# Padding three groups of matmul operand tiles by 32 bytes each, in a two-block transformer kernel

## The chip, the cores and the metric

The kernel runs on one core of a Trainium2 chip. The metric is the device time of one execution in microseconds (us). TensorE (PE) does the matmuls and loads its stationary operands (PEld), VectorE (DVE) and ScalarE (ACT) do the work on elements, SyncE (SP) issues the DMAs.

## The reference, cut to what matters

Two blocks of two layers each over 512 tokens of width 1024, all in float32. The first block's layers have forgetting, dilated and banded attention with gated branches; the second block's have a differential-attention and pooling mixer or a convolution mixer, then cross attention to 256 memory tokens and an MLP of width 4096. Nearly all of the work is matrix products of this form:

```python
u = jnp.einsum('bsd,dc->bsc', h, w_in[layer])          # first block, 6660 columns
x = x + jnp.einsum('bsd,de->bse', merged, w_out[layer])
...
proj = h @ w_in                                         # second block's mixers
q = (h @ wq).reshape(B, S, X_HEADS, X_HEAD_DIM)         # cross attention
a = jax.nn.relu(h @ w1)                                 # MLP
return (a * a) @ w2
```

## The kernel before

Every float32 operand of a product is split into two halves, a rounded high one and the rest as a low one, and a product of 128 rows of the contraction takes three matmuls: high weight by high input (line 310), high weight by low input (line 311), low weight by high input (line 312). In the usual form the weight's halves are the stationary operand (128 by 128) and the activation's halves are the moving one (128 partitions by 512 tokens); one output of 128 columns takes 8 such groups of three, one for each 128 of the 1024 rows, and all 24 matmuls add into one tile `ps_acc`.

```python
308  def mm3(self, ps, lh, ll, rh, rl, start, stop):
310      mm(ps, lh, rh, start=start, stop=False)
311      mm(ps, lh, rl, start=False, stop=False)
312      mm(ps, ll, rh, start=False, stop=stop)
...
330  def fm_into(self, ps, hi, lo, xh, xl, ks, n=S, ...):
331      for i, k in enumerate(ks):
332          c = slice((k - w0) * P, (k - w0 + 1) * P)
333          self.mm3(ps[:, :n], hi[:, c], lo[:, c], xh[k][:, :n], xl[k][:, :n], ...)
```

The weights come by DMA into `raw`, ScalarE rounds them into `whi` (line 304), and VectorE writes the rest into `wlo` (line 305); each of these has two buffers of 128 by 1024. The tiles that hold activations come from pools of their own, by `tl(tag, ...)`:

- `xhi` and `xlo`, 8 tiles each: the halves of the normalised input of a layer (lines 54 to 57). They are the moving operand of 208 weight units, 24 matmuls each: in the first block 22 units a layer for queries, keys and gates of the heads and 24 for the branch gates; in the second 12 for the even mixer, 24 for the odd one, 16 for cross attention, 64 for the MLP's first product. Of them 124 run in plain loops (36 of the branch gates, the odd mixer, the MLP) and 84 are woven between the steps of attention.
- `y`, 16 tiles, and `mg`, 16 tiles: pools that hold what goes into the second product of a layer. Where the halves are `split(..., "y", "y")`, the three matmuls of a group take y, y, y (384 groups: the branches, the two mixers' and cross attention's output products). In the MLP's second product they are `split(r, "y", "mg")` and the matmuls take y, mg, y (496 groups of 512 tokens; the last 16 groups run in halves of 256). In the first block's output product all come from mg (128 groups).
- `mg` also holds keys and values of attention and the halves of the memory, of 256 tokens; the keys are completed by DMAs from one half of the partitions to the other (lines 589 and 590).

In the products by tokens (`tm_task`, line 349) the roles are turned round: the weight's halves move, and 128 columns of an activation tile are the stationary operand, from `xhi` and `xlo` in 168 matmuls of 512 columns and from `mg` in 192.

A tile of 512 float32 takes 2048 bytes in each partition, and one of 1024 takes 4096; both are multiples of 256. So all tiles of one pool begin at the same byte modulo 256. By the order in which the pools lie in the memory, `raw`, `xhi`, `xlo`, `whi`, `wlo`, `nt`, `gt` and `RB` begin at 128, `mg`, `qk` and `cs` at 192, and `y`, `yt`, `pth` and `ptl` at 64. Slices of 128 columns (512 bytes) inside a tile begin at the same byte modulo 256 as the tile.

The order of the matmuls is written out by the program: plain loops for the large products, and in the stretches of attention a weave (lines 217 to 236) that puts the next matmuls of a list of tasks between the steps of the heads.

Of the kernel before, what the change touches and what calls it, by code (L numbers as in the profile page):

```python
# [33 lines left out]
            gt=4, yt=1, cs=2, nt=3, sz=2, RB=2, small=16, wide=5)  # L34


class Norm:
    """Root-mean-square norm whose per-token factor is applied after the product."""

# [31 lines left out]
    def finish(self, row=True, square=False):  # L71
        """The factors come in two steps, each behind the next product that is emitted."""
        self.steps = [self.per_token] + [self.per_row] * (row or square)
        self.square = square
        self.kr.hooks = list(self.steps)
        return self
# [32 lines left out]
class Head:  # L109
    """One head's steps by stage (scores, values, the rest), each at a place in its period of the weave."""  # L110

# [6 lines left out]
class JointNorm(Norm):  # L118
    """Two norms on end: x <- norm(x) gf, then norm(x) g, from sums over x and over x gf."""

# [36 lines left out]
class Kernel:  # L157
# [15 lines left out]

# [1 line left out]
    def task(self, label, cost, gen, *aps):  # L175
        """aps: the weights that the task takes, in their order."""
        self.work.append([label, cost, gen])
        self.plan += aps
        self.prepare_ahead()
# [7 lines left out]
    def step(self):  # L187
        """The next product of the first task; false where its operands are not there yet."""
        w = self.work[0]
        try:  # L190
            c = next(w[2])
        except StopIteration:
            self.work.pop(0)
            return True
        if c is None:
            return False
        w[1] -= c
        self.due -= c
        return True
# [38 lines left out]
    def tl(self, tag, dt=F32, shape=(P, S)):  # L238
        self.n += 1
        return self.pool.tile(list(shape), dt, tag=tag, name=f"{tag}_{self.n}", bufs=BUFS[tag])  # L240

# [41 lines left out]

# [1 line left out]
    def load(self, ap):  # L285
# [28 lines left out]
    def pv(self, ps, v, hi, lo, start, stop):  # L314
        """The values' halves lie side by side in one stationary tile, or in two tiles."""
        if len(v) == 2:
            return self.mm3(ps, v[0], v[1], hi, lo, start, stop)
        mm = self.nc.tensor.matmul
        mm(ps, v[0], hi, start=start, stop=False)
        mm(ps, v[0], lo, start=False, stop=stop)  # L320

    def stack_v(self, vt, acc, rs):
        """Values of four heads of one token tile: the halves of each one side by side."""
        nc = self.nc
        v = vt.rearrange("p (h c) -> p h c", c=P)
        hi, lo, src = v[:, :, :64], v[:, :, 64:], acc.rearrange("p (h c) -> p h c", c=64)
        nc.scalar.activation(hi, src, AF.Identity, scale=rs)
        nc.vector.scalar_tensor_tensor(lo, src, rs, hi.bitcast(F32), op0=ALU.mult, op1=ALU.subtract)
# [56 lines left out]

# [1 line left out]
    def rstd_tm(self, acc, n, scale, times=None, more=None):  # L387
# [17 lines left out]
    def row_form(self, rs, n):  # L405
        """The per-token factors along the free axis, in every partition."""
        nc, nt = self.nc, n // P
        hi, lo = self.sm(nt, F32R), self.sm(nt, F32R)
        nc.vector.tensor_copy(hi, rs)
        nc.vector.tensor_tensor(lo, rs, hi.bitcast(F32), op=ALU.subtract)  # L410
        ps = self.psum("t")
        for i in range(nt):
            for part in (hi, lo):
                nc.tensor.matmul(ps[:, i * P:(i + 1) * P], part[:, i:i + 1].to_broadcast([P, P]), self.identR,
                                 start=part is hi, stop=part is lo)
        return ps
# [5 lines left out]

# [1 line left out]
    def lowest(self, out, ps, bias, nm):  # L424
        """out = -(ps + bias) and the lowest of each row."""
        self.nc.vector.tensor_tensor_reduce(out, ps, bias, -1.0, HUGE, op0=ALU.add, op1=ALU.min, accum_out=nm)  # L426

    def causal_tile(self, i, qt, kt, bias, tag=None):
        """exp(s - max) of query tile i and the reciprocals of its sums."""
        nc, mm = self.nc, self.nc.tensor.matmul  # L430
        n = P * (i + 1)
        q = slice(i * P, (i + 1) * P)
        bias, masked = bias
        ps = self.psum("s")
        mm(ps[:, :n], qt[:, q], kt[0][:, :n], start=True, stop=False)
        mm(ps[:, :n], qt[:, q], kt[1][:, :n], start=False, stop=masked)
        if not masked:
            mm(ps[:, n - P:n], self.identB, self.bandB[:, P:], start=False, stop=True)
        nm, den, r = self.sm(1), self.sm(1), self.sm(1)
        p = self.tl(tag) if tag else self.tl(f"P{i}", F32, (P, n))  # L440
        self.lowest(p[:, :n], ps[:, :n], bias, nm)
        nc.scalar.activation(p[:, :n], p[:, :n], AF.Exp, scale=-1.0, bias=nm, accum_out=den)  # L442
        nc.vector.reciprocal(r, den)
        return p, r

    def causal(self, qt, kt, bias, v, done):
        """The steps of one causal head; qt, kt, bias and v are called when they are needed."""
        pr = []

        def score(i):  # L450
            p, r = self.causal_tile(i, qt(), kt(), bias(i))
            n = P * (i + 1)
            self.nc.scalar.activation(p[:, :n], p[:, :n], AF.Identity, scale=r)
            pr.append(p)

        return self.places(score), self.causal_values(pr, v, done)
# [4 lines left out]
    def causal_values(self, pr, v, done):  # L461
        """out^T[:, q] over all keys; v(j): the stationary values of key tile j."""
        nc = self.nc
# [25 lines left out]
    def band(self, qt, kt, sink, v, done):  # L489
        """The steps of one head of banded attention with a sink."""  # L490
        nc, mm = self.nc, self.nc.tensor.matmul
# [64 lines left out]

# [1 line left out]
    def z_gate(self, ap, nm):  # L558
        """z * (1 + tanh(z / 2)), twice silu(z)."""
        nc = self.nc  # L560
# [9 lines left out]
    def stack_q(self, q):  # L570
        """Queries of two heads: the halves of each one on end, over the whole contraction."""
        nc = self.nc
# [7 lines left out]
    def stack_k(self, k, tag="mg"):  # L580
        """Keys of two heads: each half of each one twice on end."""
        nc = self.nc
# [32 lines left out]
    def join(self, yt, ps, r):  # L615
        """The products of the values' two halves are added up."""
        rows = slice(64 * r, 64 * r + 64)
# [3 lines left out]
    def first_layer(self, l, nm, nxt, values_a):  # L621
# [7 lines left out]

        # forgetting attention  # L630
        acc = self.run(values_a)
# [40 lines left out]

        # forgetting attention: the decays by key, in every partition
        def decays(h):
# [15 lines left out]

        # dilated mixture and banded attention: rope tables with the norm's factor
        cs = []
# [63 lines left out]

        # gates of the branches: 1 + tanh, twice the sigmoid
        ahead = {}
# [26 lines left out]

        # gates and branches
        if l == 1:
# [73 lines left out]

# [1 line left out]
    def second_block(self, nm):  # L863
# [13 lines left out]
    def mem_norm(self):  # L877
        """In steps, each behind a product."""
        nc = self.nc
# [25 lines left out]
    def mem_halves(self, tag):  # L905
        """The normalised memory in halves: a feature chunk behind each of the next products."""
        nc, M = self.nc, 256
# [35 lines left out]
    def even_prep(self):  # L943
# [5 lines left out]

        # relative bias by distance, the longest first  # L950
        rb, oh, never = self.p1.tile([32, 4], F32, name="rb"), self.tl("nt"), self.tl("nt")
# [16 lines left out]
    def even(self, nm, nxt):  # L968
# [49 lines left out]

        # multi-scale pool
        def pool_in(g):  # L1020
# [59 lines left out]
    def begin(self, begun, w, yh, yl, ks, last):  # L1080
        """The first products of a projection, as far as their operands go."""
        for n in range(2):
# [166 lines left out]
    def finale(self, w, ah, al, nm):  # L1249
        """The last product and the last norm go by groups of tokens."""  # L1250
        nc, k = self.nc, KC - 1
# [40 lines left out]

# [1 line left out]
def _fm(w):  # L1294
    """[K, N] -> [N/128, 128, K]: for each 128 columns, the rows by chunk."""
    k, n = w.shape
# [3 lines left out]
def _tm(w):  # L1300
    """[K, n] -> [K/256, 128, 2 n]."""
    k, n = w.shape
# [115 lines left out]
```

## Time and profile before

| | us |
|---|---|
| median of 2 runs | 2299.23 (2298.43 to 2300.03) |
| span of the profiled execution | 2296.1 |
| PE busy | 2271.1 (99%) |
| PEld busy | 1870.6 (81%) |
| DVE busy | 1283.1 (56%) |
| ACT busy | 990.1 (43%) |

The span goes from the first to the last instruction of the program in the profiled execution; 3.1 us lie between it and the median of the runs. A matmul's own duration in the profile includes the time in which its result drains, while the next one already runs, so the pace of the matmuls is read from start to start.

### The profile page before, as it was taken

What the parts mean: (1) busy time and instruction counts of PE and PEld (TensorE: products, weight loads), DVE (VectorE), ACT (ScalarE), POOL (GpSimd) and SP (SyncE); (2) the same over time, 40 slices, a digit from 0 to 9 for tenths busy, and PEclk for the clock granted to TensorE, in tenths of its full rate; (3) what the DMA queues carried; (4) which work ended last, traced back from release to release, by engine and by line L of the source; (5) the groups of instructions that cost most, each with busy time, mean ns of one, the idle gap of its engine ahead of it and who ended that gap; (6) DMA issues with size and microseconds to landing.
All of it is one profiled execution on the core that took longest, in us unless ns stands there. A gap on an engine that the chain in (4) does not pass through costs nothing.

```text
span 2296.1 us, 27721 instructions
## 1 busy us (share of the span) xinstructions
PE 2271.1 (99%) x10770; PEld 1870.6 (81%) x10770; DVE 1283.1 (56%) x2212; ACT 990.1 (43%) x1672; POOL 19.6 (1%) x21
## 2 busy tenths in 40 slices
PE   8999999999999999999999999999999999999998
PEld 7888888878788888777888888888888887888887
DVE  6688654567885556885455423435455455433433
ACT  6686432366863234654443422333233443422421
POOL 0000000000000000000000000000000000000000
PEclk9999999999999999999999999999999999999999
DMA  5333233243333333323323333333333323333232
GB/s 172 92 106 94 83 95 96 93 119 98 98 104 93 92 106 106 92 83 119 102 92 92 92 101 92 100 93 106 100 93 110 111 83 94 100 93 100 92 101 83
DMA packets 74738, 227.82 MB, mean 99 GB/s; under 512 B 9928, under 2 KB 15692, under 8 KB 74608
## 3 DMA queue, kind: packets, MB, share of 16 engines
q1 hardware_dynamic: 74608, 226.06, 33.2%
q8 instruction: 84, 1.38, 0.2%
q14 instruction: 46, 0.38, 0.1%
HBM read 210.29 MB, written 2.11 MB: 93 GB/s over the span
## 4 chain that ended last, share of the span: by engine, by line
PE 86%; DVE 7%; ACT 4%; issue 1%; DMA 1%; SPq 0%; POOL 0%; DVEq 0%; POOLq 0%; ACTq 0%
PE ps_acc L310 26%; PE ps_acc L312 26%; PE ps_acc L311 26%; DVE wlo L305 2%; ACT whi L304 1%; PE ps_s L310 1%; DVE ptl L381 1%; PE ps_s L311 1%; PE ps_s L312 1%; ACT P L442 1%; PE ps_o L311 1%; PE ps_t L393 1%; PE ps_o L310 1%; PE ps_o L312 1%; DVE P L426 0%
## 5 line engine op out<-in xcount | busy, mean ns | idle before, releaser
L304 ACT CAST whi<-raw 128x1024 fp32r<-128x1024 f32 (+1 forms) x388 | 404.2, 1042 | 1009.7 <-PE ps_acc L311 671.5
L310 PE MATMUL ps_acc<-xhi,whi 128*128 128x512 f32 x1664 | 661.2, 397 | 0.0
L312 PE MATMUL ps_acc<-xhi,wlo 128*128 128x512 f32 x1664 | 650.4, 391 | 0.0
L311 PE MATMUL ps_acc<-xlo,whi 128*128 128x512 f32 x1664 | 649.2, 390 | 0.0
L305 DVE TENSOR_TENSOR wlo<-raw,whi 128x1024 fp32r<-128x1024 f32 (+1 forms) x388 | 470.8, 1213 | 281.4 <-ACT whi L304 280.3
L312 PEld LDWEIGHTS ps_acc<-xhi,wlo 128*128 128x128 f32 x1664 | 312.6, 188 | 66.4
L310 PEld LDWEIGHTS ps_acc<-xhi,whi 128*128 128x128 f32 x1664 | 313.3, 188 | 59.8 <-issue 1.3
L311 PEld LDWEIGHTS ps_acc<-xlo,whi 128*128 128x128 f32 x1664 | 313.2, 188 | 58.7 <-issue 0.5
L312 PE MATMUL ps_acc<-y,wlo 128*128 128x512 f32 (+1 forms) x912 | 356.7, 391 | 1.1 <-DVE wlo L305 1.1
L310 PE MATMUL ps_acc<-y,whi 128*128 128x512 f32 (+1 forms) x912 | 356.5, 392 | 1.2 <-ACT y L383 0.8
L311 PE MATMUL ps_acc<-mg,whi 128*128 128x512 f32 (+1 forms) x784 | 288.8, 368 | 0.0
L312 PEld LDWEIGHTS ps_acc<-y,wlo 128*128 128x128 f32 x912 | 171.2, 188 | 41.3 <-DVE wlo L305 2.4
L310 PEld LDWEIGHTS ps_acc<-y,whi 128*128 128x128 f32 x912 | 171.4, 188 | 40.9 <-ACT whi L304 1.6
L311 PEld LDWEIGHTS ps_acc<-mg,whi 128*128 128x128 f32 x784 | 147.3, 188 | 27.2
L419 DVE TENSOR_TENSOR x<-x,ps_acc 128x512 f32<-128x512 f32 x79 | 54.3, 687 | 192.4 <-PE ps_acc L312 192.4
L311 PE MATMUL ps_acc<-y,whi 128*128 128x512 f32 x384 | 152.0, 396 | 0.0
L1234 DVE SCALAR_TENSOR_TENSOR gt<-ps_acc,RB 128x512 f32<-128x512 f32 x64 | 44.3, 692 | 169.3 <-PE ps_acc L312 167.7
L380 ACT CAST pth<-ps_t 128x512 fp32r<-128x512 f32 (+1 forms) x112 | 58.5, 527 | 72.0 <-PE ps_t L540 22.6
L311 PEld LDWEIGHTS ps_acc<-y,whi 128*128 128x128 f32 x384 | 72.2, 188 | 17.3 <-DVE y L381 0.4
L310 PE MATMUL ps_acc<-mg,whi 128*128 128x512 f32 (+1 forms) x256 | 86.2, 337 | 0.0
L312 PE MATMUL ps_acc<-mg,wlo 128*128 128x512 f32 (+1 forms) x256 | 85.7, 335 | 0.0
L765 DVE TENSOR_TENSOR gt<-ps_acc,RB 128x512 f32<-128x512 f32 x36 | 24.9, 692 | 106.4 <-PE ps_acc L312 106.4
(265 smaller groups left out, 2530.7 us busy)
## 6 DMA issues: line engine op xcount, KB each, us to landing
raw<-in_w_dram SPq DMA_DIRECT2D x128, 512.0 KB, 3.6
raw<-in_w_fm_dram SPq DMA_DIRECT2D x92, 512.0 KB, 3.6
raw<-in_conv_fm_dram SPq DMA_DIRECT2D x24, 512.0 KB, 3.6
raw<-in_w_br_dram SPq DMA_DIRECT2D x16, 512.0 KB, 3.6
raw<-in_w_out_dram SPq DMA_DIRECT2D x16, 512.0 KB, 3.6
raw<-in_xk_dram SPq DMA_DIRECT2D x16, 512.0 KB, 3.6
raw<-in_xv_dram SPq DMA_DIRECT2D x16, 512.0 KB, 3.6
raw<-in_xq_dram SPq DMA_DIRECT2D x16, 512.0 KB, 3.6
```

The lines of the kernel that those rows point to most:

```text
L304: nc.scalar.copy(hi[:, :f], raw[:, :f])
L305: nc.vector.tensor_tensor(lo[:, :f], raw[:, :f], hi[:, :f].bitcast(F32), op=ALU.subtract)
L310: mm(ps, lh, rh, start=start, stop=False)
L311: mm(ps, lh, rl, start=False, stop=False)
L312: mm(ps, ll, rh, start=False, stop=stop)
L380: nc.scalar.copy(hi, src)
L381: nc.vector.tensor_tensor(lo, src, hi.bitcast(F32), op=ALU.subtract)
L393: nc.tensor.matmul(ps[:, i:i + 1], a[:, i * P:(i + 1) * P], self.ones[:, 0:1], start=a is parts[0] and i == 0, stop=a is parts[-1] and i = ...
L419: self.nc.vector.tensor_tensor(self.x[k], self.x[k], ps, op=ALU.add)
L442: nc.scalar.activation(p[:, :n], p[:, :n], AF.Exp, scale=-1.0, bias=nm, accum_out=den)
L765: nc.vector.tensor_tensor(th, ps, nm.RB, op=ALU.mult)
L1234: nc.vector.scalar_tensor_tensor(r, ps, 0.0, nm.RB, op0=ALU.max, op1=ALU.mult)
```

## The change

`tl` allots 520 columns in place of 512 for the tags `xhi`, `y` and `mg`, and gives back the first 512. A tile then takes 2080 bytes, 32 more than a multiple of 256, and the tiles of one pool begin at eight different places modulo 256. The 8 tiles of `xhi` take 256 bytes more in all, those of `y` and `mg` 512 each. These are multiples of 256, so every other tile, and the first tile of each of the three pools, begins at the same byte modulo 256 as before. `xlo`, `whi` and `wlo` stay as they were. Apart from that the change takes out docstrings and comments.

```diff
+STEPPED = ("xhi", "y", "mg")
+
...
     def tl(self, tag, dt=F32, shape=(P, S)):
         self.n += 1
+        if tag in STEPPED:
+            return self.pool.tile([P, S + 8], dt, tag=tag, name=f"{tag}_{self.n}", bufs=BUFS[tag])[:, :S]
         return self.pool.tile(list(shape), dt, tag=tag, name=f"{tag}_{self.n}", bufs=BUFS[tag])
```

## Rows read from the trace of the kernel before

**Rows 1.** The page: busy time by engine, and the span in 40 slices.
```profile
PE 2271.1 (99%) x10770; PEld 1870.6 (81%) x10770; DVE 1283.1 (56%) x2212; ACT 990.1 (43%) x1672; POOL 19.6 (1%) x21
...
PE   8999999999999999999999999999999999999998
...
PEclk9999999999999999999999999999999999999999
```

**Rows 2.** The page: the chain of work that ended last, by engine.
```profile
PE 86%; DVE 7%; ACT 4%; issue 1%; DMA 1%; SPq 0%; POOL 0%; DVEq 0%; POOLq 0%; ACTq 0%
```

**Rows 3.** Groups of matmuls by line and shape: count, busy us, mean ns.
```profile
L310 PE MATMUL ps_acc<-xhi,whi 128*128 128x512 f32 x1664 | 661.2, 397 | 0.0
L312 PE MATMUL ps_acc<-xhi,wlo 128*128 128x512 f32 x1664 | 650.4, 391 | 0.0
L311 PE MATMUL ps_acc<-xlo,whi 128*128 128x512 f32 x1664 | 649.2, 390 | 0.0
...
L310 PE MATMUL ps_acc<-y,whi 128*128 128x512 f32 x880 | 347.4, 395 | 1.2 <-ACT y L383 0.8 <-ACT whi L304 0.4
...
L311 PE MATMUL ps_acc<-mg,whi 128*128 128x512 f32 x624 | 244.2, 391 | 0.0
...
L311 PE MATMUL ps_acc<-y,whi 128*128 128x512 f32 x384 | 152.0, 396 | 0.0
...
L310 PE MATMUL ps_acc<-mg,whi 128*128 128x512 f32 x128 | 50.2, 392 | 0.0
...
L310 PE MATMUL ps_acc<-whi,mg 128*128 128x512 f32 x64 | 25.7, 401 | 0.0
...
L310 PE MATMUL ps_acc<-whi,xhi 128*128 128x512 f32 x56 | 23.0, 411 | 0.0
```

**Rows 4.** Stretches of one kind: length, busy us and count by engine, granted clock, DMA.
```profile
1411.05:1498.10 87.05, 87.05 (x385) 72.07 (x384) 40.44 (x47) 34.15 (x47) 0.00 (x0) 1.00 0.33 97
1600.00:1719.00 119.00, 119.00 (x526) 98.54 (x526) 63.84 (x83) 34.64 (x44) 0.00 (x0) 1.00 0.33 97
1719.28:1764.08 44.80, 44.80 (x193) 35.91 (x192) 24.16 (x30) 16.93 (x23) 0.00 (x0) 1.00 0.33 95
843.64:887.60 43.96, 43.96 (x193) 36.06 (x192) 28.92 (x37) 22.03 (x31) 0.00 (x0) 1.00 0.29 96
1322.30:1410.80 88.50, 88.50 (x384) 71.88 (x383) 25.77 (x25) 17.95 (x18) 0.00 (x0) 1.00 0.32 95
887.60:903.70 16.10, 16.10 (x72) 13.33 (x71) 6.32 (x7) 5.01 (x6) 0.00 (x0) 1.00 0.41 110
```

**Rows 5.** Timeline of PE where one kind of product gives way to another.
```profile
1085.94 0.39 PE L312 MATMUL ps_acc<-whi,mg 128*128 128x512 f32 x1
...
1087.34 0.40 PE L312 MATMUL ps_acc<-whi,mg 128*128 128x512 f32 x1
1087.57 0.40 PE L310 MATMUL ps_acc<-xhi,whi 128*128 128x512 f32 x1
...
1089.19 0.39 PE L311 MATMUL ps_acc<-xlo,whi 128*128 128x512 f32 x1
```

**Rows 6.** Timeline of PE behind a wait, in the first stretch of attention.
```profile
29.79 0.40 PE L311 MATMUL ps_acc<-xlo,whi 128*128 128x512 f32 x1
...
32.10 0.39 PE L312 MATMUL ps_acc<-xhi,wlo 128*128 128x512 f32 x1
```

**Rows 7.** Writers and readers of the padded tiles on other engines and queues.
```profile
L381 DVE TENSOR_TENSOR ptl<-ps_t,pth 128x512 fp32r<-128x512 f32 x76 | 52.2, 687 | 16.1 <-ACT pth L380 15.9
...
L381 DVE TENSOR_TENSOR mg<-gt,y 128x512 fp32r<-128x512 f32 x64 | 44.3, 692 | 2.7 <-ACT y L380 2.7
...
L57 DVE SCALAR_TENSOR_TENSOR xlo<-x,c_vec,xhi 128x512 fp32r<-128x512 f32 x56 | 41.7, 748 | 2.1 <-ACT xhi L56 2.1
...
mg<-mg SPq DMA_DIRECT2D x56, 128.0 KB, 2.7
```

## Prediction

> **What bounds the kernel now.** I read the page's busy times first, then its chain, then the groups of matmuls, and last the pace of the matmuls stretch by stretch. PE is busy for 99% of the span, in every slice but the two ends, at the full granted clock (the 2.4 GHz level) [rows 1], and the chain that ended last is PE for 86% [rows 2]. DVE at 56% and ACT at 43% have slack. So the change can matter only through PE: through the time from one matmul's start to the next.
>
> The groups say how many matmuls of 512 columns there are [rows 3]: 3 x 1664 = 4992 whose moving operands are xhi, xlo, xhi; 384 groups of y, y, y (1152 matmuls); 496 groups of y, mg, y (1488); 128 groups of mg, mg, mg (384). With the weights moving there are 3 x 56 = 168 against xhi and xlo, and 3 x 64 = 192 against mg. Together 8376.
>
> Their durations, 390 to 411 ns, overlap; the pace is in the stretches that hold one kind each [rows 4]. A count there includes one matmul already under way, so the pace is the length over the count less one. At 2.4 GHz 512 columns take 213.3 ns. The x kind runs at 87.05 / 384 = 226.7 ns, and in another layer at 119.00 / 525 = 226.7; y, y, y at 44.80 / 192 = 233.3; mg at 43.96 / 192 = 229.0; y, mg, y at 88.50 / 383 = 231.1; weights against xhi at 16.10 / 71 = 226.8. The weights against mg run at (1087.34 - 1085.94) / 6 = 0.233 us [rows 5]. No idle time stands before these groups [rows 3], and the granted clock is the same in all [rows 4]. What differs is where the tiles begin modulo 256 bytes: weights and x at 128, mg at 192, y at 64. The last two paces are the telling ones: the same moving tiles whi and wlo, 226.8 ns against a stationary tile that begins at the same byte and 233.3 against one that begins 64 bytes further. The pace goes with the place of the moving tile relative to the stationary one: same place 226.7, moving tile 64 bytes further 229.0, 64 bytes less 233.3 (both y against weights and weights against mg).
>
> There is a second effect. After a disturbance the x kind doesn't run at 226.7 at once. From 1087.57 to 1089.19, where x follows another kind, seven spacings take 1.62 us, 231.4 ns each [rows 5]; behind a wait, from 29.79 to 32.10, ten take 2.31 us, 231.0 ns each [rows 6]. So 226.7 is a pace into which a row of like-placed matmuls settles after some ten of them.
>
> **The change part by part.** No instruction, wait or DMA is added or taken away, and no step moves in a queue. Only places change: xhi, y and mg tiles are spread over eight places, whi, wlo and xlo stay at 128. So 24 matmuls of one unit no longer have one relation to their weights: the order goes xhi (one of eight places), xlo (the old place), xhi, and on to the next of eight.
>
> I cost this with the pace of rows in which the relation changes from matmul to matmul. There is one such kind, y, mg, y, at 231.1 ns, and the unsettled stretches of x give 231.0 and 231.4. So I take 231.1 for all kinds after the change. The bounds are the best and the dearest settled pace, 226.7 and 233.3, as the trace has no odd multiple of 32 bytes.
>
> - x in plain loops: 124 units x 24 = 2976 matmuls x (231.1 - 226.7) = +13.1 us; bounds 0 and 2976 x 6.6 = +19.6.
> - x in the weaves: 84 units x 24 = 2016. They are interrupted by attention steps and are now partly unsettled, as in rows 6, so their change lies between 0 and 4.4 ns. I take the middle, 2.2: +4.4 us; bounds 0 and 2016 x 4.4 = +8.9.
> - y, y, y: 1152 x (231.1 - 233.3) = -2.5 us; bounds 1152 x (226.7 - 233.3) = -7.6 and 0.
> - y, mg, y: it mixes two places today and eight afterwards: 0; bounds 1488 x (226.7 - 231.1) = -6.5 and 1488 x 2.2 = +3.3.
> - mg, mg, mg: 384 x (231.1 - 229.0) = +0.8 us; bounds -0.9 and +1.7.
> - weights moving: 168 x 4.3 - 192 x 2.2 = +0.3 us; bounds -1.3 and +1.1.
> - Other engines: the same subtraction takes 687 ns into ptl, which begins at 64, and 692 into mg at 192, so a place moves 0.7% of an operation that lies beside PE; I cost it at nothing, covered by the 44% of the span that DVE is idle [rows 1, 7]. If DVE were the bound, 1283.1 x 0.7% = 9 us would be the price. Likewise xlo is made by DVE in 748 ns from xhi. The 56 copies into mg take 2.7 us each and are issued tasks ahead of their use; a tenth more would be 0.3 us each, nothing where they are hidden, and at most 56 x 0.3 = 15 us if none were. I take nothing.
>
> Sum: 13.1 + 4.4 - 2.5 + 0 + 0.8 + 0.3 = +16.1 us. On the profiled span, 2296.1 + 16.1 = 2312.2; the median of the runs stands 3.1 above the span, so 2315.
>
> The rows on whi against xhi and against mg show that the stationary tile's place counts. The Trainium skill, "TensorE: Matmul & The Clock Gate", section "Step-by-step: what each phase is for", says that PE reads its moving and its stationary operand through two independent ports, so that loading the next weights takes no read bandwidth from the running matmul. By that rule alone the two paces would be equal and the sum 0, which gives 2299; the trace does not agree (226.8 against 233.3), so I keep the sum.
>
> **The rivals.**
>
> A. Faster: the steps take the tiles out of each other's way, and every kind runs at the best settled pace. For it: the place is worth 6.6 ns a matmul, and one choice of places has the low price. Against it: that low price belongs to equal places of moving and stationary tile, which the change gives up for seven of eight tiles of xhi, while it leaves the weights in place. Its price: the lower bounds, with the weaves' 2016 x -2.2 = -4.4: 0 - 4.4 - 7.6 - 6.5 - 0.9 - 1.3 = -20.7 us, 2278. If it also took away what every settled pace has over 213.3 ns, it would give 8376 x 13.4 = 112 us more, 2166; nothing in the rows points there, since all its pairings stay above 226.
>
> B. Slower than forecast: a tile that begins at an odd multiple of 32 bytes is as bad for its matmuls as the dearest pairing. It decides if the unknown places lie above the mean of the known ones. Upper bounds: 19.6 + 8.9 + 0 + 3.3 + 1.7 + 1.1 = +34.6 us, 2334. If an odd place cost 6.6 ns beyond what a mixed pace has, half of the moving tiles from the three pools would pay it: (2 x 1664 + 1152 + 1488 + 384) / 2 = 3176 x 6.6 = 21 us on top of 16, 2336; on top of the 34.6 it would be 2355. Against it: nothing in the rows sets odd multiples apart, and they lie between places that are cheap and dear.
>
> C. The change does nothing: the place counts only in units larger than 32 bytes, or the paces differ for another reason (kind of product, tile of the output), and the mean over eight places happens to be today's. Time 2299. The Trainium skill has a rule that leads there: "SBUF — State Buffer", section "Door 1: The DMA port swizzle", says that the memory is read in lines of 16 bytes and that only crossing to a new line costs; a step of 32 bytes keeps every tile at the start of a line, so by that rule no matmul changes. The trace speaks against it: 64, 128 and 192 all begin a line, and they run at three paces.
>
> **How the numbers follow.** Chances: forecast 0.48 (with its own range 2305 to 2325), A 0.20, B 0.20, C 0.12. The predicted time is the forecast's, 2315. The range takes in C, B's first price and A's price, since cases of both signs are open: 2276 to 2337; outside remain A's tail below and B's second price above. A measurement of this kernel tells from no change about 2%, that is 2253 to 2345. Faster than that is only A's tail, 0.03; slower only B's sum of both prices, 0.05; the same 0.92.
>
> **What would show it.** In the profile after, the stretches of the MLP's first product (385 matmuls in 87.05 us today) should be some 1.7 us longer, at 231 ns a matmul; that of y, y, y (44.80 us) about 0.4 us shorter; those of y, mg, y unchanged. Durations of DVE and ACT should stay within 1%, and the counts and waits should be as before. The forecast is wrong if the x kind still settles at 226.7 (rival A or C), or if some kind runs above 233.3 for a whole unit (rival B); a pace below 226 anywhere would mean that the step does something that no pairing of today shows. The weakest step is that one pace stands for all eight places, with xlo and the weights unmoved.

## The result, and the profile after

The changed kernel takes 2317.97 us (median of 2 runs, 2316.27 to 2319.67) against 2299.23 (2298.43 to 2300.03): a ratio of 1.0082, 95% interval 1.0052 to 1.0111. It is slower, by 18.7 us. The profiled execution is the slower of the two: its span is 2317.9 us and the other's 2314.5, against 2296.1 before.

First the page of the changed kernel: busy time by engine, the granted clock by slice, and the chain by engine.

```profile
PE 2293.0 (99%) x10770; PEld 1873.7 (81%) x10770; DVE 1283.7 (55%) x2212; ACT 990.6 (43%) x1672; POOL 19.6 (1%) x21
...
PEclk9999999999999999999999999999999999999999
...
PE 88%; DVE 6%; ACT 3%; issue 1%; DMA 1%; SPq 0%; POOL 0%; DVEq 0%; POOLq 0%; ACTq 0%
```

Counts are those of before, and DVE and ACT took 0.6 and 0.5 us more in all [rows 1]. PE's busy time grew by 21.9 us, the span by 21.8: the time is in PE, and not in a wait. The groups by line and shape (count, busy us, mean ns; the lines stand four further down than before) show where to look: the three of xhi and xlo are longer by 4 ns each [rows 3], while the subtraction into ptl and mg took 686 and 693 ns against 687 and 692 [rows 7].

```profile
L314 PE MATMUL ps_acc<-xhi,whi 128*128 128x512 f32 x1664 | 667.0, 401 | 0.0
L316 PE MATMUL ps_acc<-xhi,wlo 128*128 128x512 f32 x1664 | 656.9, 395 | 0.0
L315 PE MATMUL ps_acc<-xlo,whi 128*128 128x512 f32 x1664 | 655.6, 394 | 0.0
...
L385 DVE TENSOR_TENSOR ptl<-ps_t,pth 128x512 fp32r<-128x512 f32 x76 | 52.2, 686 | 15.9 <-ACT pth L384 15.6
L385 DVE TENSOR_TENSOR mg<-gt,y 128x512 fp32r<-128x512 f32 x64 | 44.3, 693 | 2.7 <-ACT y L384 2.7
```

The pace itself is in the stretches of one kind, as in rows 4 (length; busy us and count of PE, PEld, DVE, ACT, POOL; granted clock, DMA share, GB/s). The stretches of the changed kernel are, in this order: x in the MLP, x in the convolution mixer, y,y,y, mg, y,mg,y, weights against xhi, weights against mg. In each, one matmul of the count was already under way, and the pace is length by count less one.

```profile
1423.55:1512.28 88.73, 88.73 (x384) 71.92 (x384) 40.55 (x47) 34.03 (x46) 0.00 (x0) 1.00 0.32 95
1614.63:1736.50 121.87, 121.87 (x527) 98.79 (x527) 63.81 (x83) 34.67 (x44) 0.00 (x0) 1.00 0.31 95
1736.73:1781.08 44.35, 44.35 (x192) 35.86 (x192) 24.16 (x30) 16.76 (x23) 0.00 (x0) 1.00 0.30 95
850.30:894.55 44.25, 44.25 (x192) 35.87 (x192) 28.92 (x37) 21.87 (x30) 0.00 (x0) 1.00 0.31 96
1334.59:1423.32 88.73, 88.73 (x384) 71.90 (x384) 25.78 (x25) 17.74 (x18) 0.00 (x0) 1.00 0.31 95
894.78:911.19 16.41, 16.41 (x72) 13.34 (x72) 6.32 (x7) 4.81 (x6) 0.00 (x0) 1.00 0.33 112
1788.27:1799.15 10.88, 10.88 (x48) 8.81 (x48) 4.76 (x6) 4.81 (x6) 0.00 (x0) 1.00 0.57 188
```

So x went from 226.7 to 88.73 / 383 = 231.7 ns (121.87 / 526 = 231.7 in the mixer); y,y,y from 233.3 to 232.2; mg from 229.0 to 231.7; y,mg,y from 231.1 to 231.7; weights against xhi from 226.8 to 231.1, and against mg from 233 to 231.5 [rows 4, 5]. Before, the kinds ran at paces from 226.7 to 233.3; now all are within 1.1 ns of each other. In an x unit the timeline of PE (start, duration) has 24 spacings in 5.56 us, 231.7 ns each, with nothing between the matmuls.

```profile
1435.88 0.39 PE L314 MATMUL ps_acc<-xhi,whi 128*128 128x512 f32 x1
...
1441.44 0.39 PE L314 MATMUL ps_acc<-xhi,whi 128*128 128x512 f32 x1
```

The row PEclk shows 9 in every slice, but the clock was not granted in full everywhere. In both traces it fell to the 1.2 GHz level (0.50) at PE waits of 0.69 and 0.78 us ahead of a y,y,y unit, and at one of 0.88 us ahead of an x unit. The rows are y,y,y and x of the kernel before, then y,y,y of the changed one:

```profile
1022.64:1023.92 1.28, 1.28 (x4) 0.99 (x3) 0.61 (x2) 0.41 (x1) 0.00 (x0) 0.50 0.36 102
1936.90:1938.61 1.71, 1.71 (x5) 1.32 (x4) 0.69 (x1) 0.93 (x2) 0.00 (x0) 0.50 0.64 208
1031.15:1034.99 3.84, 3.84 (x10) 2.97 (x9) 1.40 (x3) 0.66 (x2) 0.00 (x0) 0.50 0.28 73
```

All of these matmuls take some 427 ns, whatever their places. In those two units seven spacings ran so before (three of y,y,y, four of x) and fifteen after (ten and five). Eight more, at some 195 ns extra each, are about 1.6 us of the 21.8. The stretches compared in this document all have a granted clock of 1.00, except where 0.50 is shown.

### The profile page after: what moved, and what is told of

It is laid out like the page before. It is cut to its first block, busy times and chain, and to the rows that moved or that the text cites. A ratio compares the mean times of both kernels' runs of the same rounds, so it can differ in the third digit from the quotient of the medians.

```text
span 2317.9 us, 27721 instructions
## 1 busy us (share of the span) xinstructions
PE 2293.0 (99%) x10770; PEld 1873.7 (81%) x10770; DVE 1283.7 (55%) x2212; ACT 990.6 (43%) x1672; POOL 19.6 (1%) x21
## 4 chain that ended last, share of the span: by engine, by line
PE 88%; DVE 6%; ACT 3%; issue 1%; DMA 1%; SPq 0%; POOL 0%; DVEq 0%; POOLq 0%; ACTq 0%
PE ps_acc L314 27%; PE ps_acc L316 27%; PE ps_acc L315 27%; DVE wlo L309 1%; PE ps_s L314 1%; ACT whi L308 1%; PE ps_s L315 1%; PE ps_s L316 1%; DVE ptl L385 1%; ACT P L446 1%; PE ps_o L315 1%; PE ps_o L314 1%; PE ps_t L397 1%; PE ps_o L316 1%; PE ps_t L475 1%
```

## The experiments

The theories that they were to tell apart, by the numbers that the expectations use. Theory 1: the pace goes by the place of the moving tile less that of the stationary one, modulo 256 bytes, with a cheap pace at equal places into which only a row of equal relations settles. Theory 2: the moving tile's own place counts. Theory 3: the kind of product counts, not the place. Theory 4: odd multiples of 32 bytes are dear in themselves. Theory 5: the loss lies in y and mg. After the first four runs came theory 6, on mixed rows: each matmul has the settled price of its own relation. With the last two came theory 7, places count in blocks of 32 bytes, and theory 8, only exactly equal places are cheap.

All kernels are edits of the kernel before. Those that have one time and no interval were run once; the kernel before, run beside them, took 2297.4 to 2303.0 us. "Gap" is an empty tile that is allotted ahead of the first tile of a tag, so that it and all behind it move:

```python
+    def gap(self, tag):
+        if tag in GAPS:
+            self.n += 1
+            self.pool.tile([P, GAPS.pop(tag) // 4], F32, tag=f"gap_{tag}", name=f"gap_{self.n}", bufs=1)
+
     def tl(self, tag, dt=F32, shape=(P, S)):
+        self.gap(tag)
         self.n += 1
```

In the fences below the columns are those of the stretches above, and the paces are worked out in the same way. The stretches that one kind of product fills are the same ones in every kernel: the MLP (x), the mixer's output product (y,y,y), and the first block's output product (mg).

### e1: every operand at the same place

```diff
+GAPS = dict(mg=192, P3=128)
```

mg, y, qk, pth and ptl then begin at 128, as the weights and x do.

> Every tile unstepped as before, but two empty gaps put y, mg, qk, pth and ptl at 128 modulo 256, the place of the weights and of x. Theory 1 (the pace goes with the place of the moving tile relative to the stationary one, and a row of equal relations settles): y,y,y falls from 233.3 to 226.7 ns a matmul, y,mg,y from 231.1 to 226.7, mg,mg,mg from 229.0 to 226.7, weights against mg from 233.3 to 226.7, x stays at 226.7; sum -16 us and a little more in attention, 2278 to 2285. Theory 2 (the moving tile's own place sets the pace, whatever the stationary tile's): the same for the first three, but weights against mg stay at 233.3, 2284. Theory 3 (the kind of product sets the pace, not the place): nothing changes, 2299.

Measured: 2283.07 us (median of 5 runs, 2282.95 to 2284.34), a ratio of 0.9931, interval 0.9917 to 0.9944. The stretches of this kernel, x, y,y,y, mg, y,mg,y and a short one of weights against mg:

```profile
1405.03:1491.85 86.82, 86.82 (x384) 71.89 (x384) 40.45 (x47) 33.96 (x46) 0.00 (x0) 1.00 0.32 97
1711.55:1754.85 43.30, 43.30 (x192) 35.85 (x192) 24.16 (x30) 16.78 (x23) 0.00 (x0) 1.00 0.31 97
840.41:883.70 43.29, 43.29 (x192) 35.84 (x192) 28.92 (x37) 21.86 (x30) 0.00 (x0) 1.00 0.32 97
1317.99:1404.81 86.82, 86.82 (x384) 71.89 (x384) 25.76 (x25) 17.82 (x18) 0.00 (x0) 1.00 0.31 97
1838.69:1841.86 3.17, 3.17 (x15) 2.62 (x15) 1.17 (x2) 1.64 (x2) 0.00 (x0) 1.00 0.47 143
```

All five run at 226.7 ns (3.17 / 14 = 226.4, within what two decimals show). The kinds of product keep their weights, lines and waits, so theory 3 falls. The saving, 16.0 us against the kernel before in the same runs, is what the old paces say: 1152 x 6.6 + 1488 x 4.4 + 384 x 2.3 + 192 x 6.6 = 16.3 us. By the sizes of the pools in their order, x and mg here lie an even multiple of 256 bytes from the weights and y an odd one, and the paces are equal: 256 bytes more or less make no difference.

### e2 and e3: odd multiples of 32 bytes, settled

```diff
+GAPS = dict(xhi=32, whi=224, mg=160, qk=96, y=192)      # e2
+GAPS = dict(xhi=96, whi=160, mg=96, qk=160, y=64)       # e3
```

e2 puts x 32 bytes further than the weights, mg 32 less and y 128 away; e3 puts x 96 further, mg 96 less and y at the weights' place. The weights stay at 128.

> Unstepped, weights at 128, but xhi and xlo begin 32 bytes further than the weights, mg 32 bytes less, y 128 bytes away. Theory 1: settled paces between those of the neighbouring places, x between 226.7 and 229.0 ns, mg between 226.7 and 233.3, y,y,y between 229.0 and 233.3; time 2297 to 2308. Theory 4 (odd multiples of 32 bytes are dear in themselves): x and mg at 233 ns or above, time 2325 or above.

> Unstepped, weights at 128, but xhi and xlo begin 96 bytes further than the weights, mg 96 bytes less, y at the same place as the weights. Theory 1: x between 229 and 233 ns, mg about 232 to 233, y,y,y at 226.7; time 2300 to 2316. Theory 2: the same, but it has no reason for 226.7 of y,y,y beyond its own place at 128. Theory 4: x and mg at 233 or above, 2325 or above.

Measured: e2 2326.03 us and e3 2324.12. The stretches x, mg and y,y,y of e2:

```profile
1428.31:1517.66 89.35, 89.35 (x384) 71.80 (x384) 40.51 (x47) 34.02 (x46) 0.00 (x0) 1.00 0.31 95
853.29:897.85 44.56, 44.56 (x192) 35.89 (x192) 28.92 (x37) 21.90 (x30) 0.00 (x0) 1.00 0.31 95
1742.80:1787.36 44.56, 44.56 (x192) 35.85 (x192) 24.16 (x30) 16.75 (x23) 0.00 (x0) 1.00 0.30 95
```

And the same three of e3:

```profile
1427.03:1516.40 89.37, 89.37 (x384) 71.91 (x384) 40.66 (x47) 34.15 (x46) 0.00 (x0) 1.00 0.32 95
851.64:896.38 44.74, 44.74 (x192) 35.98 (x192) 28.92 (x37) 21.90 (x30) 0.00 (x0) 1.00 0.32 94
1742.00:1785.32 43.32, 43.32 (x192) 35.85 (x192) 24.16 (x30) 16.78 (x23) 0.00 (x0) 1.00 0.32 98
```

x 32 and x 96 bytes further: 233.3 each; mg 32 less 233.3, 96 less 234.2; y 128 away 233.3, at the same place 226.8. My reading between known places (226.7 to 229 for 32 bytes) was wrong: as settled paces, odd multiples are all dear. This agrees with theory 4 (e2's time is in its range, e3's 0.9 us under it), though not with it alone, since 64 less (y in the kernel before) and 128 away, both even, are as dear.

### e4: the weights moved, x, y and mg left

```diff
+GAPS = dict(whi=64, nt=192)
```

whi and wlo begin at 192; no moving tile of an x, y or mg product is anywhere else than before.

> Unstepped; whi and wlo begin 64 bytes further (192), all other tiles as before. Theory 1: x now lies 64 bytes less than the weights and slows from 226.7 to 233.3 ns; mg,mg,mg has the weights' place and falls from 229.0 to 226.7; y,y,y lies 128 away and has the pace that it has in the first scan; time about 2299 + 2976 x 6.6 ns + 2016 x 4.4 ns, less some 3, 2322 to 2328. Theory 2: no kind with y, mg or x moving changes, 2299.

Measured: 2318.28 us. The stretches x, mg, y,y,y and weights against xhi of this kernel:

```profile
1423.32:1512.68 89.36, 89.36 (x384) 72.01 (x384) 40.63 (x47) 34.04 (x46) 0.00 (x0) 1.00 0.30 95
852.15:895.49 43.34, 43.34 (x192) 35.86 (x192) 28.92 (x37) 21.85 (x30) 0.00 (x0) 1.00 0.34 98
1737.00:1781.38 44.38, 44.38 (x192) 35.98 (x192) 24.17 (x30) 16.77 (x23) 0.00 (x0) 1.00 0.29 95
895.76:911.78 16.02, 16.02 (x71) 13.15 (x70) 6.30 (x7) 4.76 (x6) 0.00 (x0) 1.00 0.38 110
```

x, unmoved, now runs at 233.3 and mg, unmoved too, at 226.9; y, now 128 away, at 232.4. The same moving bytes run at another pace when the stationary tile goes elsewhere, x slower and mg faster, so theory 2 falls and the relation stands. The weights moving, now 64 bytes further than xhi, run at 228.9, the 229.0 that mg had before at 64 further. The total came out below the 2322 to 2328 expected.

### e5 and e6: one part of the change alone

```diff
+STEPPED = ("xhi",)          # e5
+STEPPED = ("y", "mg")       # e6
```

> One part of the change: only xhi is stepped by 32 bytes, y and mg stay. Theory 1: x runs at the pace of the changed kernel, 231.7 ns in plain loops; 2976 x 5.0 = 14.9 us, some 5 in the weaves and 0.7 where x is stationary; 2317 to 2321. Theory 5 (the loss is in y and mg): 2299 to 2301.

> The other part: only y and mg are stepped. Theory 1: y,y,y 231.7 to 232.2 in place of 233.3, y,mg,y 231.5 in place of 231.1, mg,mg,mg 232 in place of 229; terms -1.5, +0.6 and +1.1 us, 2298 to 2301. Theory 5: 2314 or above.

Measured: e5 2315.99 us (median of 4 runs, 2315.52 to 2316.73), ratio 1.0069, interval 1.0052 to 1.0086; e6 2300.89 us (median of 10, 2299.22 to 2303.51), ratio 1.0006, interval 0.9996 to 1.0015. The stretches x and y,y,y of e5:

```profile
1421.25:1509.98 88.73, 88.73 (x384) 71.93 (x384) 40.51 (x47) 34.02 (x46) 0.00 (x0) 1.00 0.31 95
1734.21:1778.78 44.57, 44.57 (x192) 35.72 (x192) 24.13 (x30) 16.79 (x23) 0.00 (x0) 1.00 0.31 95
```

And mg, x and y,y,y of e6:

```profile
845.14:889.39 44.25, 44.25 (x192) 35.88 (x192) 28.91 (x37) 21.89 (x30) 0.00 (x0) 1.00 0.32 95
1413.66:1500.51 86.85, 86.85 (x384) 71.88 (x384) 40.44 (x47) 33.94 (x46) 0.00 (x0) 1.00 0.31 97
1722.17:1766.51 44.34, 44.34 (x192) 35.86 (x192) 24.14 (x30) 16.79 (x23) 0.00 (x0) 1.00 0.32 96
```

Each part has the paces of the whole change in its own kinds (x 231.7; y,y,y 232.1 and mg 231.7) and those of before in the others (233.3; 226.8). Against the kernel before in the same runs, 2299.33, they are +16.7 and +1.6 us, together 18.2 of the 18.7. e5 came out 1.0 us under the 2317 to 2321 expected; e6 is in its range, and its interval takes in no change. The loss is xhi's, and theory 5 falls.

### e7 and e10: xhi stepped by 128 and by 64 bytes

```diff
+STEPPED = ("xhi",)
...
+            return self.pool.tile([P, S + 32], ...)[:, :S]      # e7
+            return self.pool.tile([P, S + 16], ...)[:, :S]      # e10
```

xhi then takes two places (e7) or four (e10), none of them an odd multiple of 32 bytes from the weights.

> Only xhi is stepped, by 128 bytes: four of its eight tiles have the weights' place, four lie 128 bytes away, where the first scan has 233.3 ns; xlo has the weights' place. Theory 6 (each matmul has the settled price of its own relation): x at (24 - 8 x ... ) that is 16 of 24 at 226.7 and 8 at 233.3, 228.9 ns, 2306 to 2310. Theory 1 with settling (a row in which the relation changes has a pace of its own, near 231): x at 230 to 232, 2314 to 2320.

> Only xhi is stepped, by 64 bytes: two tiles each at 0, 64, 128 and -64 bytes from the weights, no odd multiple of 32. Theory 6 (each matmul has its relation's settled price): high halves (226.7 + 229.0 + 233.3 + 233.3) / 4 = 230.6, low halves 226.7, together 229.3 ns, 2306 to 2310. Theory 1 with settling (any change of relation costs): 230.0, as with steps of 128, to 231.7, as with steps of 32; 2309 to 2318.

Measured: e7 2308.42 us, e10 2314.72. The stretch x of e7, and behind it that of e10:

```profile
1416.98:1505.07 88.09, 88.09 (x384) 71.88 (x384) 40.52 (x47) 33.99 (x46) 0.00 (x0) 1.00 0.32 96
```

```profile
1420.02:1508.54 88.52, 88.52 (x384) 71.88 (x384) 40.57 (x47) 34.06 (x46) 0.00 (x0) 1.00 0.32 95
```

That is 230.0 and 231.1 ns. With four places and no odd multiple the kind already pays nearly all that eight places cost (231.7). So odd multiples aren't what makes the changed kernel slow, although they are dear when settled: theory 4 doesn't explain the result. Theory 6 had 228.9 and 229.3, which is 1.1 and 1.8 ns too low: these mixed rows of x cost more than the mean of their settled prices. e7 doesn't decide between the two by itself: its pace is theory 1's (230 to 232), but its time, 2308.42, lies in theory 6's 2306 to 2310 and under theory 1's 2314. e10 does: its time is out of theory 6's 2306 to 2310 and in theory 1's 2309 to 2318, and its pace is in the latter's 230.0 to 231.7.

### e8: the same place for all, elsewhere

```diff
+GAPS = dict(xhi=32, mg=192, P3=128)
```

All operands begin at 160, an odd multiple of 32 bytes.

> As the kernel with all operand tiles at one place, but that place is 160 modulo 256 (an odd multiple of 32) in place of 128. Theory 1 (the relation alone counts): all kinds at 226.7 ns, 2280 to 2286, as at 128. Theories 2 and 4 (the place itself counts, odd multiples are dear): 233 ns and above, 2335 or above.

Measured: 2283.41 us (median of 4 runs, 2283.12 to 2283.6), ratio 0.9927, interval 0.9912 to 0.9941. The stretches x, y,y,y and mg of this kernel:

```profile
1405.38:1492.20 86.82, 86.82 (x384) 71.89 (x384) 40.58 (x47) 33.99 (x46) 0.00 (x0) 1.00 0.32 97
1711.90:1755.20 43.30, 43.30 (x192) 35.85 (x192) 24.15 (x30) 16.79 (x23) 0.00 (x0) 1.00 0.33 98
840.45:883.74 43.29, 43.29 (x192) 35.84 (x192) 28.92 (x37) 21.88 (x30) 0.00 (x0) 1.00 0.32 97
```

These are the lengths of e1 to the hundredth. The odd place 160 is as good as 128 as long as both operands have it: of the two, neither counts by itself, the relation does.

### e9: the weights 16 bytes further

```diff
-        hi = self.tl("whi", F32R, (P, D))
-        lo = self.tl("wlo", F32R, (P, D))
+        hi = self.tl("whi", F32R, (P, D + 64))[:, 4:4 + D]
+        lo = self.tl("wlo", F32R, (P, D + 64))[:, 4:4 + D]
```

> Unstepped, tiles of activations as before; whi and wlo begin 16 bytes further than before (144), so x lies 16 bytes less than the weights, mg 48 more, y 80 less. Theory 7 (the price goes by blocks of 32 bytes: 128 and 144 lie in one block): x stays at 226.7 ns, y,y,y at 233.3, mg at 229.0, about 2299. Theory 8 (only equal places are cheap, at any distance): x at 229 to 234, like the 32 byte steps of the first scan, 2305 to 2328.

Measured: 2317.44 us. The stretches x of the MLP, x of the convolution mixer, y,y,y and mg of this kernel:

```profile
1423.52:1512.88 89.36, 89.36 (x384) 72.36 (x384) 40.69 (x47) 34.11 (x46) 0.00 (x0) 1.00 0.32 95
1615.07:1734.29 119.22, 119.22 (x527) 98.75 (x527) 63.81 (x83) 34.62 (x44) 0.00 (x0) 1.00 0.33 97
1734.34:1778.65 44.31, 44.31 (x192) 35.85 (x191) 24.16 (x30) 16.93 (x23) 0.00 (x0) 1.00 0.32 96
850.18:894.46 44.28, 44.28 (x192) 35.83 (x191) 28.92 (x37) 22.04 (x30) 0.00 (x0) 1.00 0.31 95
```

The same relation, x 16 bytes less than the weights, ran at 89.36 / 383 = 233.3 in one layer and at 119.22 / 526 = 226.7 in another. y,y,y ran at 232.0 and mg at 231.8, where theory 7 had 233.3 and 229.0. So theory 7 is right for x in the mixer alone, and theory 8 for the rest. The layer doesn't decide, as PE's timeline shows within the mixer:

```profile
1608.63 0.39 PE L312 MATMUL ps_acc<-xhi,wlo 128*128 128x512 f32 x1
...
1613.53 0.39 PE L312 MATMUL ps_acc<-xhi,wlo 128*128 128x512 f32 x1
1613.76 1.01 PE L414 MATMUL ps_t<-cc_identR,sm 128*128 128x128 f32 x8
1614.61 0.44 PE L310 MATMUL ps_acc<-xhi,whi 128*128 128x512 f32 x1
1614.89 0.39 PE L311 MATMUL ps_acc<-xlo,whi 128*128 128x512 f32 x1
...
1616.93 0.39 PE L311 MATMUL ps_acc<-xlo,whi 128*128 128x512 f32 x1
```

The 21 spacings up to 1613.53 are 233.3 ns each; behind eight small matmuls the nine from 1614.89 on are 226.7, and the row keeps that pace to the end of the mixer, over weights that alternate between two buffers. So both are paces into which a row of one relation can settle, and which one it takes changed here at an interruption. What in the interruption decides is open.

## Why the prediction was right

**The mechanism.** The relation of the moving to the stationary tile was the right reading of rows 4 and 5, and the runs show it: the weights moved alone (e4) change the pace of unmoved x, mg and y, and equal places give 226.7 to every kind, at either of two places (e1, e8). That 226.7 is a pace into which a row settles is supported, not proved: x alternating between a cheap place and others runs at 230.0 to 231.7 with two, four or eight places (e7, e10, e5), and e9's row keeps a pace until something interrupts it.

**The sum by terms.** One pace of 231.1 for all kinds was taken; 231.1 to 232.2 was measured.
- x in plain loops: predicted +13.1 us, measured 2976 x (231.7 - 226.7) = +14.9.
- x in the weaves: predicted +4.4. The starts of all 4992 x matmuls of the two traces, added up, give 1159.8 us before and 1178.6 after, +18.8; less the 14.9 this leaves +3.9, 1.9 ns each where 2.2 was taken.
- y,y,y: predicted -2.5, measured by the pace 1152 x (232.2 - 233.3) = -1.3. Its starts, added up, give -0.1: seven more of them ran at the 1.2 GHz level, 7 x 195 = +1.4.
- y,mg,y: predicted 0. The stretch above gives 1488 x 0.6 = +0.9, another had 0.2 ns; the starts give +0.5.
- mg: predicted +0.8, measured by the pace 384 x 2.7 = +1.0, by the starts +1.2.
- Weights moving: predicted +0.3 for 168 and 192 matmuls. Against xhi and xlo there are 288 of 512 columns, not 168: the rows counted those that write `ps_acc`, and 120 more write `ps_s`, `ps_o` and `ps_t`. The starts give +0.6 and -0.3, together +0.3.
- Not in the sum: 192 matmuls with the weights moving in 260 columns, by the starts +0.6, and 480 with y or mg moving in 256 columns, +0.5.

By the starts, 18.8 - 0.1 + 0.5 + 1.2 + 0.3 + 0.6 + 0.5 = +21.8 us, which is what the profiled span grew by; all other matmuls together changed by -0.1. The sum had 16.1. The mis-sized terms are x in plain loops (0.6 ns a matmul, 1.8 us), y,y,y (2.4 us, of which the clock is 1.4), and the narrower matmuls, which the sum left out (1.1 us). The matmuls at the 1.2 GHz level don't go with the places: e6, which steps y and mg, has three spacings of y,y,y there as the kernel before has, and e1, with equal places, nine. The span came out 5.7 us above the predicted 2312.2 and the median 3.0 above 2315, since the median takes in the other execution, whose span is 3.4 us shorter.

**The engines beside PE.** Costing them at nothing holds: DVE and ACT are unchanged, and the waits too. The copies from mg to mg took 3.0 us against 2.7 [rows 7], by the table of DMA issues of the changed kernel (packets' queue, count, KB each, median us to landing):

```profile
mg<-mg SPq DMA_DIRECT2D x56, 128.0 KB, 3.0
```

But they took 2.9 and 3.1 in e5 and e4, which leave mg where it was, so this isn't put down to the places of mg; PE's time shows no wait for it.

**The rivals.** A's price, 2278, was nearly reached by e1 (2283), by equal places and not by steps: the argument against A, that the cheap pace belongs to equal places, was the right one. B is half true: odd multiples are the dear ones when settled (e2, e3), against the sentence that nothing sets them apart, which was only an absence of rows. It didn't decide, since in mixed rows they add little to what even ones cost (231.1 with e10's four places, 231.7 with eight). C falls: 32 bytes are enough to change the pace. The rule of the Trainium skill that stood under C ("SBUF — State Buffer", section "Door 1: The DMA port swizzle": only a new line of 16 bytes costs) doesn't describe this: in e2 every tile still begins a line, and the paces changed.

**Where the weak step was.** The prediction named the one pace for eight places as its weakest step. It held within 1.1 ns, but not for a reason that the runs found. The settled prices by moving less stationary place are 226.7 (0), 233.3 (+32), 229.0 (+64), 233.3 (+96), 232.4 to 233.3 (128), 234.2 (-96), 233.3 (-64) and 233.3 (-32), a mean of some 232.0. With xlo still at 0, a third of the x matmuls would pay 226.7, and the mean would be (2 x 232.0 + 226.7) / 3 = 230.2, less than the 231.7 measured. So a mixed row has a pace of its own. It can also lie below the mean: y,mg,y had 231.1 where its settled prices have a mean of 231.9, and in e2 and e4 (the stretches follow) it had 231.1 and 228.9 against means of 233.3 and 230.6.

```profile
1339.38:1427.90 88.52, 88.52 (x384) 72.17 (x383) 25.77 (x25) 17.91 (x18) 0.00 (x0) 1.00 0.32 95
1335.24:1422.91 87.67, 87.67 (x384) 71.84 (x383) 25.78 (x25) 17.93 (x18) 0.00 (x0) 1.00 0.31 96
```

The prediction took its one pace from a single mixture; as others differ by over 2 ns, that it came so near is in part luck. Which of the two operands' reads is held up, if either, stays open: no run here took the weight load away from a matmul. Open too is why even 226.7 lies above 213.3, half of the 426.7 ns that y,y,y takes at the 1.2 GHz level.

## What to carry to other kernels

Where TensorE is busy for 99% of the span, read its pace from start to start for each kind of product, and look at the start addresses of both operands where the paces differ: here giving the moving and the stationary tiles the same start modulo 256 bytes (two empty tiles of 192 and 128 bytes) made the kernel 0.7% faster, and spreading them made it 0.8% slower. Spreading tiles helped only the kind whose one relation was among the dearest (y,y,y, 233.3 to 232.2 ns); where the common relation was the best one (x), it cost 5.0 ns a matmul. Don't interpolate between measured places: 0 and 64 were the two cheap ones, and 32, between them, was as dear as the rest.

## What was not expected of the hardware

- The pace as a function of the relation isn't smooth: 226.7 ns at 0, 233.3 at +32, 229.0 at +64, 233.3 at +96, and 232.4 to 234.2 at the others.
- One relation can have two settled paces: with x 16 bytes less than the weights, 233.3 ns through the MLP and 226.7 through most of the convolution mixer, within one execution, with the change at an interruption (e9).
- At the 1.2 GHz level no price of the place shows: y,y,y, 64 bytes less than the weights, and x, at the same place, both took some 427 ns a matmul in the kernel before.
- Two places of xhi in place of one cost x 3.3 ns a matmul, half of the dearest settled difference of 6.6, although only 8 of the 24 matmuls of a unit leave the cheap relation (e7, 230.0).
